# A decoder trunk on one core: the third attention unit is turned by DMA, one step's weights are split first, and GpSimd's work on a convolution channel is put behind another unit's low parts

## The chip, the cores and the metric

The kernel runs on one core of a Trainium2 chip. The core has a matrix engine (TensorE, "PE" in the profile), three engines for elementwise work (VectorE "DVE", ScalarE "ACT", GpSimd "POOL") and a queue engine (SyncE "SP") that issues most transfers. Each engine works its own instruction queue in order; semaphores make one wait for another. The metric is the device time of one execution in microseconds (us), lower is better.

## The reference

Two layers over 512 tokens of width 1024, float32 throughout. Each layer is a half-weighted SwiGLU block, a mixing block and another half-weighted SwiGLU block, with a norm ahead of each. The change lies in the mixing block:

```python
h = rms_norm(x, mix_norm[l])
z = h @ w_in[l]                      # [q | k | v | conv_B | conv_C | conv_h]
# attention: 8 query heads, 2 key/value heads of 64, blocks of 128 tokens,
# each block sees itself and the block before (window 128), ALiBi bias, a learned sink
scores = einsum(qb, k_band) * scale + bias        # masked
m = maximum(max(scores), sink);  p = exp(scores - m)
probs = p / (sum(p) + exp(sink - m))
out = einsum(probs, v_band)
# convolution: B * causal_conv3(C * h_conv), per channel
x = x + concat([attn_out, conv_out]) @ w_out[l]
```

## The kernel before

Every matrix product is made from three products of a short format: both operands are split into a high part (a cast on ScalarE, `wh` for weights) and a low part (the rest, a subtraction on VectorE, `wl`), and high x high, low x high and high x low are summed in PSUM. `split` (line 228) does it for weights; `need_raw` loads them (line 210 on SP), and `need_split(g)` splits all groups up to the g-th. `wh` and `wl` have three buffers each, the loaded weights (`raw`) eight, which they share with the attention's probabilities `p`.

The mixing block goes in steps. One step has a group of 24 products of 128 by 512 columns on TensorE (the function `group`, lines 318 to 321): steps 2 to 5 make the queries, steps 6 to 17 the twelve 128-wide pieces of the convolution's three inputs, in two rounds of six: C for two channels (`cc`, line 1700), h for two channels (`ch`, line 1707, then the three taps), B for two channels (`m`, line 1720). So steps 8 and 9 are `ch` of channels 0 and 1, steps 10 and 11 the products with B. The taps' sum `cc` gets an addition and a product with the norm on GpSimd (lines 1715 and 1716).

Between the groups lies the attention, cut into eight units, one for each block n of 128 tokens and each key/value head g: `p_n_g`, in the order 0_0, 1_0, 2_0, 3_0, 0_1, 1_1, 2_1, 3_1. A unit has four heads with 256 columns of scores (128 for block 0), and these stages:

- `scores`: products of q with the high and low part of k into PSUM (`sc`, lines 1554 and 1555); on VectorE a reduction per head that adds the bias and finds the maximum (line 1558), then `nm`, `es`; on ScalarE four exponentials and one of the sink (`es`, lines 1575 and 1578); on VectorE `sums`, a reciprocal, and the scaling of p (line 1583).
- `turn`: p is needed with keys on the partitions. On TensorE: 128-column transposes into PSUM (`pt`, line 1616). For units 1, 3 and 5 instead by DMA: in `send`, ScalarE lays the two 16-bit halves of each word apart (line 1590, into `crossing`), SP issues a DMA transpose of 16-bit elements back into p (line 1592); in `join`, ScalarE puts the halves together again, one copy for each of the two key blocks (line 1601). Either way each block is then split into `ph` (ScalarE, line 1621) and `pl` (VectorE, line 1622).
- `values`: four products with the values (`o`, lines 1633 and 1634; two for block 0), a copy of the lower half `ol` on ScalarE (line 1636) and additions on VectorE (line 1639).

At which step a unit does what stands in the tables `SCORES_AT`, `SEND_AT`, `TURN_AT`, `VALUES_AT`. `attend(step)` runs the stages of a step; `go_on` calls it, then splits the weights of a group ahead. `INSIDE` names a stage that is run inside a group, between two of its eight k. `tc.issue_after(i)` puts what stands under it behind instruction i. Within these bounds a scheduler orders each engine's instructions, by costs of its own.

PSUM has four accumulators of the kind `mm`, taken in turn by groups (`acc`) and values (`o`), and two each of `sc` and `aux`.

Of the kernel before, what the change touches and what calls it, by code (L numbers as in the profile page):

```python
# [65 lines left out]
SPLIT_AHEAD = 2  # L66
# [9 lines left out]
def trunk_kernel(  # L76
# [23 lines left out]
    nc = tc.nc  # L100
# [519 lines left out]
    norm = Norm(0)  # L620
# [873 lines left out]
    def mix(l, norm, after):  # L1494
# [40 lines left out]
        class Unit:  # L1535
# [49 lines left out]
            def send(self):  # L1585


                self.room = crossing[:, todo.index(self) // 2 % 2, :]
                halves = self.room.bitcast(U16).rearrange("p (two n) -> p two n", two=2)
                nc.scalar.copy(halves, words(self.p.rearrange("p h k -> p (h k)")))  # L1590
# [16 lines left out]
            def turn(self):  # L1607

                self.pt = []
                for kb in range(self.lo // P, 2):  # L1610
                    if todo.index(self) in SEND_AT.values():
                        tp = self.join(kb)
                    else:
                        tp = psum("aux", [P, 4, P], f"pt_{self.name}_{kb}")
                        for h in range(4):
                            nc.tensor.transpose(
                                tp[:, h, :], self.p[:, h, kb * P : (kb + 1) * P], ident
                            )
                    hi = g2(f"ph_{self.name}_{kb}", F32R, (P, 4, P))
                    lo = g2(f"pl_{self.name}_{kb}", F32R, (P, 4, P))  # L1620
                    nc.scalar.copy(hi, tp)
                    last = nc.vector.tensor_sub(lo, tp, f32(hi))
                    self.pt.append((kb, hi, lo))
                return last

# [20 lines left out]
        def attend(step):  # L1646

            done = None
            if step in SEND_AT:
                todo[SEND_AT[step]].send()  # L1650
            for at, stage in ((VALUES_AT, "values"), (TURN_AT, "turn"), (SCORES_AT, "scores")):
                if stage == "turn" and step + 1 == INSIDE[0]:
                    done = todo[VALUES_AT.index(step)].added
                    continue
                if step in at:
                    done = getattr(todo[at.index(step)], stage)() or done
            return done

        for j in range(NH // 2):
# [18 lines left out]
        def product():  # L1678

            def between(k, hi, lo):  # L1680
                if step == INSIDE[0] and k == INSIDE[2]:
                    todo[INSIDE[1]].turn()
# [13 lines left out]
        for pair in range(2):  # L1696
# [7 lines left out]
            for j in range(2):  # L1704
# [7 lines left out]
                nc.vector.scalar_tensor_tensor(  # L1712
                    tap[:, 2:], u[:, : S - 2], conv_of(l, 0, c), tap[:, 2:], op0=ALU.mult, op1=ALU.add
                )
                nc.gpsimd.tensor_add(y[:, 1:], y[:, 1:], tap[:, 1:])
                nc.gpsimd.tensor_mul(y, y, norm.inv)
# [68 lines left out]
```

## Time and profile before

| | us |
|---|---|
| median of 3 runs | 1626.99 |
| lowest, highest | 1626.22, 1627.17 |
| the profiled execution | 1626.19 |
| its span, first to last instruction | 1624.4 |
| TensorE busy | 1615.4 (99%) |
| VectorE, ScalarE, GpSimd busy | 1376.7, 1178.1, 216.5 |
| attention of layer 1, layer 2 | about 363 to 452, 1166 to 1255 |

A row of the timeline is: start (us from the span's start), duration, engine, line, operation, output<-input, shape, count; in brackets, how long the engine stood idle just before and what ended that. Several like rows are merged to "xN". A row of the waits is: who waited, for whom, us in total, times, longest. A row of the windows is: the stretch and its length, then for each engine its busy time and, in brackets, its instructions, then TensorE's granted clock, the share of the DMA engines and GB/s. Matmuls overlap, so their starts tell more than their durations.

### The profile page before, as it was taken

To read this page: it belongs to the slowest core of one execution; us is meant where nothing else is said; L and a number is where in the kernel's file an instruction comes from. 1 tells how busy PE (TensorE), PEld (TensorE's weight loads), DVE (VectorE), ACT (ScalarE), POOL (GpSimd) and SP (SyncE) were. 2 spreads that over 40 slices of the span, in tenths; PEclk is the share of its full clock that TensorE was granted. 3 is DMA by queue.
4 is the path that set the end of the run, shared out by engine and by line. 5 is a ranking of instruction groups with operands and counts; after the bars stand their busy time and mean duration, and the time that the engine had idled before them with its cause. 6 is when DMAs were issued, how large, how long until landed. Compare 5 with 4: busy or idle time off the path is not lost.

```text
span 1624.4 us, 21158 instructions
## 1 busy us (share of the span) xinstructions
PE 1615.4 (99%) x7571; PEld 1349.4 (83%) x7571; DVE 1376.7 (85%) x1788; ACT 1178.1 (73%) x1511; POOL 216.5 (13%) x191
## 2 busy tenths in 40 slices
PE   9999999999999999999999999999999999999998
PEld 7888888888898888888888888888888988888887
DVE  7978798988899977798998777989688998678997
ACT  6677777857766677778866777788586767878665
POOL 1211111001211111111011111110012111111121
PEclk9999999999999999999999999999999999999999
DMA  9999989822597698999767999998136978999892
GB/s 270 212 232 209 220 207 226 233 59 78 143 227 175 177 225 214 218 214 225 218 144 182 224 215 226 215 221 217 42 91 156 233 149 219 225 223 222 241 230 72
DMA packets 306031, 313.92 MB, mean 193 GB/s; under 512 B 125501, under 2 KB 188549, under 8 KB 305925
## 3 DMA queue, kind: packets, MB, share of 16 engines
q1 hardware_dynamic: 265412, 230.90, 50.1%
q0 software_dynamic: 40048, 81.27, 29.3%
q8 instruction: 59, 0.97, 0.2%
q14 instruction: 48, 0.39, 0.1%
q10 hardware_dynamic: 464, 0.40, 0.1%
HBM read 264.29 MB, written 2.10 MB: 164 GB/s over the span
## 4 chain that ended last, share of the span: by engine, by line
PE 98%; DVE 1%; DMA 0%; SPq 0%; issue 0%; ACT 0%; DVEq 0%
PE x L842 27%; PE y L842 13%; PE x_s L842 9%; PE acc L318 7%; PE acc L319 7%; PE acc L321 7%; PE w L842 7%; PE y_s L842 5%; PE x_m L827 3%; PE w_s L842 3%; PE y_m L827 1%; PE y_e L842 1%; PE acc L699 1%; PE x_e L842 1%; PE w_m L827 1%; PE sc L1555 0%
## 5 line engine op out<-in xcount | busy, mean ns | idle before, releaser
L228 DVE TENSOR_TENSOR wl<-raw,wh 128x1024 fp32r<-128x1024 f32 (+1 forms) x494 | 598.6, 1219 | 162.8 <-ACT wh L228 161.9
L228 ACT CAST wh<-raw 128x1024 fp32r<-128x1024 f32 (+1 forms) x494 | 514.1, 1044 | 304.6 <-PE x L842 92.8
L318 PE MATMUL acc<-xh,wh 128*128 128x512 f32 x392 | 153.3, 393 | 0.5 <-ACT wh L228 0.5
L319 PE MATMUL acc<-xl,wh 128*128 128x512 f32 x392 | 153.1, 391 | 0.0
L321 PE MATMUL acc<-xh,wl 128*128 128x512 f32 x384 | 149.7, 390 | 0.0
L223 POOL DMA_DIRECT2D raw<-in_ffn_wu_dram x40 | 50.6, 1272 | 381.6 <-DMA raw<-in_ffn_wu_dram 268.6
L318 PEld LDWEIGHTS acc<-xh,wh 128*128 128x128 f32 x392 | 73.8, 188 | 15.0 <-ACT wh L228 0.6
L319 PEld LDWEIGHTS acc<-xl,wh 128*128 128x128 f32 x392 | 73.7, 188 | 14.5
L321 PEld LDWEIGHTS acc<-xh,wl 128*128 128x128 f32 x384 | 72.1, 188 | 15.3
L223 POOL DMA_DIRECT2D raw<-in_ffn_wd_dram x34 | 41.0, 1218 | 272.0 <-DMA raw<-in_ffn_wd_dram 122.3
L223 POOL DMA_DIRECT2D raw<-in_ffn_wg_dram x40 | 49.1, 1237 | 201.9 <-DMA raw<-in_ffn_wu_dram 84.7
L269 DVE TENSOR_TENSOR raw<-raw,raw 128x1024 f32<-128x1024 f32 x58 | 70.5, 1220 | 1.7 <-DMA raw<-in_ffn_wu_dram 1.2
L1106 ACT COPY raw_a<-turned 128x1024 uint16<-128x1024 uint16 x48 | 63.5, 1357 | 0.0
L842 PE MATMUL x<-wl,ft1h 128*128 128x512 f32 x160 | 62.4, 390 | 0.0
L842 PE MATMUL w<-wh,fb21h 128*128 128x512 f32 x160 | 62.3, 390 | 0.0
L842 PE MATMUL y<-wh,ft3h 128*128 128x512 f32 x160 | 62.3, 390 | 0.0
L842 PE MATMUL x<-wh,ft1l 128*128 128x512 f32 x160 | 62.3, 389 | 0.0
L842 PE MATMUL x<-wl,ft2h 128*128 128x512 f32 x160 | 62.3, 389 | 0.0
L842 PE MATMUL x<-wh,ft2l 128*128 128x512 f32 x160 | 62.3, 389 | 0.0
L842 PE MATMUL x<-wh,ft1h 128*128 128x512 f32 x160 | 62.3, 389 | 0.0
L842 PE MATMUL w<-wh,fb21l 128*128 128x512 f32 x160 | 62.2, 389 | 0.0
L842 PE MATMUL y<-wh,ft3l 128*128 128x512 f32 x160 | 62.2, 389 | 0.0
(517 smaller groups left out, 4545.2 us busy)
## 6 DMA issues: line engine op xcount, KB each, us to landing
raw<-in_ffn_wu_dram SPq DMA_DIRECT2D x127, 512.0 KB, 5.6
raw<-in_ffn_wd_dram SPq DMA_DIRECT2D x105, 512.0 KB, 5.6
raw<-in_ffn_wg_dram SPq DMA_DIRECT2D x86, 512.0 KB, 5.3
raw<-in_ffn_wu_dram POOLq DMA_DIRECT2D x40, 512.0 KB, 9.1
raw<-in_ffn_wg_dram POOLq DMA_DIRECT2D x40, 512.0 KB, 6.5
raw<-in_w_in_dram SPq DMA_DIRECT2D x36, 512.0 KB, 4.0
raw<-in_ffn_wd_dram POOLq DMA_DIRECT2D x34, 512.0 KB, 8.2
raw<-in_w_out_dram SPq DMA_DIRECT2D x20, 512.0 KB, 4.6
```

What stands on the lines that cost most here:

```text
L223: nc.gpsimd.dma_start(out=r, in_=rows_of(*more), accum_op=ALU.add)
L228: return nc.scalar.copy(hi, raw), eng.tensor_sub(lo, raw, f32(hi))
L269: nc.vector.tensor_add(a11, a11, s1)
L318: nc.tensor.matmul(acc, hi[:, k, :], rhs[k][0], start=k == first, stop=False)
L319: nc.tensor.matmul(acc, hi[:, k, :], rhs[k][1], start=False, stop=False)
L321: nc.tensor.matmul(acc, lo[:, k, :], rhs[k][0], start=False, stop=k == last)
L699: nc.tensor.matmul(opening[n], (lo if part == "w" else hi)[:, k, :], xl if part == "x" else xh, start=n not in begun, stop=k == KC - 1 and ...
L827: nc.tensor.matmul(accs[c // 2][:, c % 2, :], w[:, k, cols], x_[:, 2 * h + k, :], start=start and c % 2 == 0 and h + k + i == 0, stop=h + ...
L842: nc.tensor.matmul(accs[u], x_[:, 2 * h + k, tok], w[:, k, :], start=start and h + k + i == 0, stop=h + k == 2 and i == 2, skip_group_chec ...
L1106: nc.scalar.copy(words(raws[self.b][:, c, :]), self.to[:, :, c, :])
```

## The change

Four edits, all in the mixing block.

1. Unit 2_0 (the third) is added to `SEND_AT`, at step 8: its eight TensorE transposes in step 9 go, and it is sent through the DMA. Its words are laid apart by GpSimd (`IDLE_LAYS`), not by ScalarE, and into half of the tile `m_1`, which is not written before the second round, instead of `crossing`. It is turned at step 10 (before: 8) and its values are made at step 11 (before: 9).
2. Unit 1_0's values move into step 11's group, ahead of its k = 3 (before: between steps 10 and 11). Unit 0_1's turn stays in that group at k = 5.
3. At step 9, `go_on` splits the weights of a coming group before the step's attention is recorded, instead of after it.
4. The GpSimd addition and product of channel 1 are recorded after step 9's attention and put behind unit 1_0's low parts (`parted`, the last `pl`).

```diff
-SEND_AT = {7: 1, 9: 3, 11: 5}
-TURN_AT = (6, 9, 8, 11, 10, 13, 14, 15)
-VALUES_AT = (7, 10, 9, 12, 11, 14, 15, 16)
-INSIDE = (11, 4, 5)
+SEND_AT = {7: 1, 8: 2, 9: 3, 11: 5}
+TURN_AT = (6, 9, 10, 11, 10, 13, 14, 15)
+VALUES_AT = (7, None, 11, 12, 11, 14, 15, 16)
+INSIDE = {(11, 3): (1, "values"), (11, 5): (4, "turn")}
+SPLIT_FIRST = 9
+IDLE_LAYS = (2,)
...
-                self.room = crossing[:, todo.index(self) // 2 % 2, :]
+                n = todo.index(self)
+                self.room = crossing[:, n // 2 % 2, :]
+                if n == 2:
+                    self.room = mixed[1][:, 2:4, :].rearrange("p c s -> p (c s)")
                 halves = self.room.bitcast(U16).rearrange("p (two n) -> p two n", two=2)
-                nc.scalar.copy(halves, words(self.p.rearrange("p h k -> p (h k)")))
+                whole = words(self.p.rearrange("p h k -> p (h k)"))
+                (nc.gpsimd.tensor_copy if n in IDLE_LAYS else nc.scalar.copy)(halves, whole)
...
-                    last = nc.vector.tensor_sub(lo, tp, f32(hi))
+                    last = self.parted = nc.vector.tensor_sub(lo, tp, f32(hi))
...
         def go_on():
             nonlocal step
+            if step == SPLIT_FIRST:
+                need_split(state["group"] - 1 + SPLIT_AHEAD)
             last = attend(step)
...
-                nc.gpsimd.tensor_add(y[:, 1:], y[:, 1:], tap[:, 1:])
-                nc.gpsimd.tensor_mul(y, y, norm.inv)
                 ys.append(y)
-                go_on()
+                behind = step == SPLIT_FIRST
+                if behind:
+                    go_on()
+                with tc.issue_after(todo[1].parted.ins) if behind else nullcontext():
+                    nc.gpsimd.tensor_add(y[:, 1:], y[:, 1:], tap[:, 1:])
+                    nc.gpsimd.tensor_mul(y, y, norm.inv)
+                if not behind:
+                    go_on()
```

What it does to the order, in the first layer (the second has the same). Numbers at the end of names tell buffers apart and differ between the two programs, as line numbers do.

On VectorE at steps 8 and 9, before: unit 2_0 and unit 3_0 are handled in turn, with the two subtractions of unit 2_0 (`pl`, from PSUM) and the weights behind `nm_3_0`.

```order
L1712 SCALAR_TENSOR_TENSOR tap_0_3422<-ch_0_0_3394,par,tap_0_3422 128x510
L1622 TENSOR_TENSOR pl_2_0_0_3433<-pt_2_0_0_3427,ph_2_0_0_3432 128x512
L1558 ISA p_3_0_3446,mx_3_0_3445<-sc_3_0_1_3454,bias,sink 128x256
L1558 ISA mx_3_0_3445 128x1
L1622 TENSOR_TENSOR pl_2_0_1_3442<-pt_2_0_1_3436,ph_2_0_1_3441 128x512
L1569 TENSOR_SCALAR nm_3_0_3461<-mx_3_0_3445 128x4
L228 TENSOR_TENSOR wl_3480<-raw_3126,wh_3479 128x1024
```

The same place in the changed kernel:

```order
L1585 TENSOR_SCALAR p_2_0_3357<-p_2_0_3357,sums_2_0_3376 128x256 x4
L1721 SCALAR_TENSOR_TENSOR tap_0_3422<-ch_0_0_3394,par,tap_0_3422 128x510
L1560 ISA p_3_0_3430,mx_3_0_3429<-sc_3_0_1_3438,bias,sink 128x256
L1560 ISA mx_3_0_3429 128x1
L230 TENSOR_TENSOR wl_3501<-raw_3164,wh_3500 128x1024
L1571 TENSOR_SCALAR nm_3_0_3445<-mx_3_0_3429 128x4
L1573 TENSOR_TENSOR es_3_0_3447<-sink,nm_3_0_3445 128x4
```

The two subtractions of 2_0 are gone from here, and weights one group further on (`wl_3501`) now stand ahead of `nm_3_0`; the weights that stood behind `nm_3_0`, from `raw_3126`, stand a step earlier, ahead of `nm_2_0`.

On GpSimd, the changed kernel (before, the first of these rows was not there):

```order
L1596 COPY m_1_2959<-p_2_0_3357 128x2048
L1729 TENSOR_TENSOR cc_0_0_3246<-cc_0_0_3246,tap_0_3422 128x511
L1730 TENSOR_TENSOR cc_0_0_3246<-cc_0_0_3246,inv_3011 128x512
L1729 TENSOR_TENSOR cc_0_1_3320<-cc_0_1_3320,tap_1_3495 128x511
L1730 TENSOR_TENSOR cc_0_1_3320<-cc_0_1_3320,inv_3011 128x512
```

The copy of 2048 16-bit elements reads `p_2_0` as soon as it is scaled, and channel 0's two operations follow it.

On ScalarE at steps 9 to 11, before, from the laying apart of 3_0 to the cast `ph_0_1_1` that `o_0_1` reads:

```order
L1590 COPY crossing_3080<-p_3_0_3446 128x2048
L1621 CAST ph_1_0_1_3533<-crossing_3080 128x512
L228 CAST wh_3644<-raw_3314 128x1024
L228 CAST wh_3704<-raw_3388 128x1024
L1575 ACTIVATE p_0_1_3538,sums_0_1_3557<-p_0_1_3538,nm_0_1_3553 128x128 x4
L1578 ACTIVATE es_0_1_3555<-es_0_1_3555 128x4
L1636 COPY ol_1_0_3606<-o_1_0_3601 64x512
L1601 COPY crossing_3080<-p_3_0_3446 128x2x512 x2
L1621 CAST ph_0_1_1_3669<-pt_0_1_1_3664 128x512
```

and in the changed kernel:

```order
L1577 ACTIVATE p_0_1_3517,sums_0_1_3536<-p_0_1_3517,nm_0_1_3532 128x128 x4
L1580 ACTIVATE es_0_1_3534<-es_0_1_3534 128x4
L1607 COPY m_1_2959<-p_2_0_3357 128x2x512 x2
L1627 CAST ph_2_0_0_3577<-m_1_2959 128x512
L1607 COPY crossing_3080<-p_3_0_3430 128x2x512
L1627 CAST ph_2_0_1_3582<-m_1_2959 128x512
L1607 COPY crossing_3080<-p_3_0_3430 128x2x512
L1642 COPY ol_1_0_3639<-o_1_0_3634 64x512
L1577 ACTIVATE p_1_1_3587,sums_1_1_3606<-p_1_1_3587,nm_1_1_3602 128x256 x4
L1580 ACTIVATE es_1_1_3604<-es_1_1_3604 128x4
L1627 CAST ph_0_1_1_3654<-pt_0_1_1_3649 128x512
```

Between the exponentials of 0_1 and `ph_0_1_1` stand now the joins and casts of unit 2_0 and the exponentials of unit 1_1; before, these exponentials came behind it. On TensorE, the products `o_2_0`, two score products of unit 2_1 and the first product of `o_0_1` now stand behind step 11's group, and the second of `o_0_1` behind the first three products of step 12's.

More of the change, by code (lines that the diff above doesn't have):

```diff
@@ L1651, in attend @@
             for at, stage in ((VALUES_AT, "values"), (TURN_AT, "turn"), (SCORES_AT, "scores")):
[L1652 to L1656, printed above, removed]
+                for n in (n for n, when in enumerate(at) if when == step):
+                    if (n, stage) in INSIDE.values():
+                        done = todo[1].parted
+                    else:
+                        done = getattr(todo[n], stage)() or done
             return done
@@ L1680, in between @@
             def between(k, hi, lo):
-                if step == INSIDE[0] and k == INSIDE[2]:
-                    todo[INSIDE[1]].turn()
+                if (step, k) in INSIDE:
+                    n, stage = INSIDE[step, k]
+                    getattr(todo[n], stage)()
             return group(norm.h, between, own=take_split(SPLIT_AHEAD - 1))
```

## The prediction

> **What bounds the kernel now.** I read the page first, then TensorE's waits, then the attention stage of the first layer (363 to 452 us) engine by engine in the timeline, and two windows to see that the second layer repeats it.
>
> ```profile
> span 1624.4 us, 21158 instructions
> PE 1615.4 (99%) x7571; PEld 1349.4 (83%) x7571; DVE 1376.7 (85%) x1788; ACT 1178.1 (73%) x1511; POOL 216.5 (13%) x191
> ...
> PE 98%; DVE 1%; DMA 0%; SPq 0%; issue 0%; ACT 0%; DVEq 0%
> ```
> ```profile
> PE idle L151 <- DVE warm L646: 1.2, 1, 1.2
> PE xt L665 <- DMA xin<-in_x_dram: 0.6, 1, 0.6
> PE acc L318 <- ACT wh L228: 0.5, 1, 0.5
> ```
> ```profile
> 363.00:452.00 89.00, 89.00 (x441) 74.25 (x440) 73.39 (x195) 63.63 (x131) 15.76 (x12) 1.00 0.42 113
> 1166.00:1255.00 89.00, 89.00 (x444) 74.63 (x443) 74.00 (x196) 64.06 (x131) 15.44 (x12) 1.00 0.42 113
> ```
>
> TensorE carries the time: the chain is 98% PE, its three waits come to 2.3 us, and in both attention windows it is busy for all 89.00 us at clock 1.00 with 441 and 444 products. So this change can win only what it takes off TensorE, and every us in which TensorE waits is lost. VectorE (73.39 of 89) and ScalarE (63.63) have slack on average; what counts is one chain through them.
>
> What the change takes off TensorE, and the place where it will be measured:
>
> ```profile
> 389.81 1.12 PE L1616 MATMUL pt<-ident,p 128*128 128x128 f32 x8
> 390.69 0.48 PE L319 MATMUL acc<-xl,wh 128*128 128x512 f32 x1
> ...
> 403.08 0.39 PE L1633 MATMUL o<-ph,vv 128*128 128x512 f32 x1
> 403.43 0.50 PE L1634 MATMUL o<-pl,vv 128*128 128x512 f32 x1
> ...
> 410.67 0.39 PE L1633 MATMUL o<-ph,vv 128*128 128x512 f32 x1
> 410.90 0.39 PE L1634 MATMUL o<-pl,vv 128*128 128x512 f32 x1
> 411.13 0.39 PE L318 MATMUL acc<-xh,wh 128*128 128x512 f32 x1
> ```
>
> The eight transposes of unit 2_0 hold TensorE from 389.81 to 390.69, 0.88 us, and the product behind takes 0.48 where others take 0.39: 0.97 us. The last product of o_1_0 starts 0.35 behind its neighbour where 0.23 is usual (410.90 to 411.13), since pl_1_0_1 was late: 0.12 us. At 411.13 the group of step 12 begins; I compare the two kernels there.
>
> **The change part by part.** *The bound of the gain.* Without the transposes and that wait TensorE is 0.97 + 0.12 = 1.09 us ahead per layer, 2.2 us in all, if nothing new holds it.
>
> *What now stands behind the new copy.* GpSimd takes over the copy that lays unit 2_0's words apart, 2048 uint16 in a partition, once p_2_0 is scaled. The trace has no such copy on GpSimd. These rows bound it and show what else it does:
>
> ```profile
> 0.27 0.10 POOL L1772 MEMSET const-float32-1.0<- 128x1 f32 x1
> ...
> 0.88 0.21 POOL L171 MEMSET ones<- 128x128 f32 x1
> ...
> 1.36 0.29 POOL L173 CAST ones_r<-ones 128x128 fp32r<-128x128 f32 x1
> 345.04 1.04 POOL L1675 TENSOR_TENSOR inv<-inv 128x512 f32<-128x512 f32 x1 [59.89 <-DVE inv L447]
> ...
> 399.82 1.29 POOL L1715 TENSOR_TENSOR cc<-cc,tap 128x511 f32<-128x511 f32 x1 [4.79 <-issue]
> 401.19 1.63 POOL L1716 TENSOR_TENSOR cc<-cc,inv 128x512 f32<-128x512 f32 x1
> ```
> ```profile
> 385.50 0.17 DVE L1569 TENSOR_SCALAR nm<-mx 128x4 f32<-128x4 f32 x1
> 387.92 0.16 DVE L1579 TENSOR_TENSOR sums<-sums,es 128x4 f32<-128x4 f32 x1 [2.05 <-ACT es L1578]
> 389.19 1.13 DVE L1583 TENSOR_SCALAR p<-p,sums 128x256 f32<-128x256 f32 x4
> 391.48 0.75 DVE L1712 SCALAR_TENSOR_TENSOR tap<-ch,par,tap 128x510 f32<-128x510 f32 x1 [0.34 <-ACT tap L1711]
> 394.98 1.21 DVE L228 TENSOR_TENSOR wl<-raw,wh 128x1024 fp32r<-128x1024 f32 x1
> 400.48 1.18 DVE L1622 TENSOR_TENSOR pl<-crossing,ph 128x512 fp32r<-128x512 f32 x1
> 402.40 0.97 DVE L1622 TENSOR_TENSOR pl<-crossing,ph 128x512 fp32r<-128x512 f32 x1
> 413.88 0.69 DVE L1622 TENSOR_TENSOR pl<-crossing,ph 128x512 fp32r<-128x512 f32 x1
> ```
>
> The same subtraction takes 0.69 us alone (413.88) and 1.18 and 0.97 beside GpSimd. It ends 0.55 behind GpSimd's end both times: 401.66 behind 399.82 + 1.29 = 401.11, and 403.37 behind 401.19 + 1.63 = 402.82. In between GpSimd's own product is the late one, 1.63 for 1.29, and ends 1.16 behind VectorE's 401.66. So of the two, whoever comes second stands until the first is through, if VectorE reads two operands from SBUF. [...]
>
> The length of the copy: the cast of 128 elements takes 0.29, of which the fixed part lies between the 0.10 of a one-column memset and the 0.21 of a memset of the same 128. That leaves 1.5 to 0.6 ns an element, 3.1 to 1.5 us for 2048. ScalarE does the very copy in 1.90 (383.02, below); four times GpSimd's 1.04 for 512 elements of a product is 4.2. I take 2.4, the middle of what GpSimd's own one-operand row gives, with 1.5 and 4.2 as ends. [...] No row here shows a long copy on GpSimd.
>
> *When it runs.* Step 8 now has weights (wl_3464) split ahead of nm_2_0, so nm_2_0 starts about 1.0 later (a wl takes 1.21, and small instructions start just before the end of what stands ahead). The exponentials shift with it, the sums from 387.92 to 389.1 with a score reduction now in front of them, and p_2_0 is scaled from 390.1 to 391.25, 1.0 behind the sums because two more reductions lie between (before: 389.19 to 390.32). tap_0, with two SBUF operands, starts next and ends at 391.9; the copy gets its turn there and ends at 391.9 + 2.4 - 0.14 = 394.2. Next but one on VectorE is wl_3501 with two SBUF operands, ready at 392.2: it stands until 394.2 and ends 1.08 (1.21 - 0.14) later, at 395.3. Behind it in VectorE's queue stand nm_3_0, es_3_0 and ch_0_1; ScalarE's exponentials of unit 3_0 wait for nm_3_0 and start at 395.4.
>
> *The chain on ScalarE.* From there ScalarE never gets free before the unit that TensorE wants next:
>
> ```profile
> 383.02 1.90 ACT L1590 COPY crossing<-p 128x2048 uint16<-128x2048 uint16 x1 [0.30 <-DVE p L1583]
> ...
> 395.10 0.51 ACT L1575 ACTIVATE p<-p,nm 128x256 f32<-128x256 f32 x1 [1.33 <-DVE nm L1569]
> ...
> 397.18 0.71 ACT L1709 ACTIVATE cc<-ch,par 128x512 f32<-128x512 f32 x1
> ...
> 398.52 0.59 ACT L1636 COPY ol<-o 64x512 f32<-64x512 f32 x1
> ...
> 399.53 1.90 ACT L1590 COPY crossing<-p 128x2048 uint16<-128x2048 uint16 x1
> 401.33 0.62 ACT L1621 CAST ph<-crossing 128x512 fp32r<-128x512 f32 x1
> 401.85 1.99 ACT L228 CAST wh<-raw 128x1024 fp32r<-128x1024 f32 x2
> 403.75 0.40 ACT L1575 ACTIVATE p<-p,nm 128x128 f32<-128x128 f32 x1
> ...
> 405.41 0.57 ACT L1636 COPY ol<-o 64x512 f32<-64x512 f32 x1
> 405.88 2.57 ACT L1601 COPY crossing<-p 128x1024 uint16<-128x1024 uint16 x2
> 408.78 0.59 ACT L1621 CAST ph<-pt 128x512 fp32r<-128x512 f32 x1 [0.33 <-PE pt L1616]
> ```
>
> Before, the cast ph_0_1_1 (408.78) ends at 409.37, and o_0_1 runs at 410.67 without waiting. In the new order ScalarE does, from the exponentials of 3_0 to the end of ph_0_1_1, start to start: exponentials and es 2.08; cc and tap 1.34 (397.18 to 398.52); ph 0.5; wh 0.95; lay of 3_0 1.80; ph 0.5; exponentials of 0_1 1.66; two joins of 2_0 2.45; ph 0.5; join 1.23; ph 0.5; join 1.23; ol_1_0 0.47; exponentials of 1_1, now ahead, 2.08; ph_0_1_1 0.59. That is 17.9 us, so ph_0_1_1 ends at 395.4 + 17.9 = 413.3. GpSimd spares ScalarE the 1.90 us that laying 2_0 apart would have cost it; new in ScalarE's list are the two joins (2.45), and the 2.08 that now stand in front of ph_0_1_1.
>
> *The sum.* TensorE comes to o_0_1 at 410.67 - 1.09 + 0.24 (two score products that moved ahead) = 409.8, or a little later, since p_0_1 is scaled late for its transposes. It waits until 413.3, some 3 us, and starts step 12 one product later, 413.5, against 411.13. One product of o_0_1 (0.23) is still owed there, two score products (0.24) are done: even. So +2.4 us a layer, +4.8 in all. The profiled execution took 1626.2 (span 1624.4 and 1.8 around it), the median is 1627.0, 0.8 above; 1627.0 + 4.8 = 1631.8. Each us of the copy is 2 us of the total: 1.5 gives +3.0, 4.2 gives +8.4.
>
> *The other edits.* The convolution's add and product for channel 1 now follow pl_1_0_1: the two subtractions get back 0.49 and 0.28 us of VectorE, which is waiting for ScalarE there, so nothing; their result is done by about 407 and wanted by step 11's product at about 411. Those of channel 0 wait behind the copy and wl_3501 until 395.3 and are done by 398; step 10's product needs them at 404. On SP one more transpose stands ahead of that of 3_0, which is not ready before 402, and ahead of two weight loads whose slots come free with the joins, at 407 and 410; their casts come three steps later. With o_1_0, o_2_0 and o_0_1 together, the accumulator of step 12 is now that of step 11, read by VectorE at about 412: hidden while TensorE waits for ph_0_1_1, late next if that goes.
>
> **The rivals.** [...] *B: not slower, the transposes' time is won.* ScalarE would have to finish ph_0_1_1 by 410, 3.3 us earlier than in my sum; that needs the copy out of the way and 1.5 us of slack in ScalarE's list which I don't see. From 410 on the price is nil, and 1627.0 - 2.2 = 1624.8. *C: the copy is as slow as GpSimd's two-operand rows*, 4.2 us: +8.4, 1635.4. The joins, at 406 and later, would still find their transpose landed. [...] Against it: a copy reads one operand, not two.
>
> **How the numbers follow.** My forecast (copy 1.6 to 3 us) 0.44, C and anything longer 0.18, A 0.22, B 0.16. 0.2% is 3.3 us, about what a measurement here tells from no change; a copy of 1.65 us reaches it. Slower: 0.44 + 0.18 = 0.62. Same: A and B, less a little for what I have not seen, 0.36. Faster by 3.3 us is more than the transposes hold: 0.02. The range from 1627.0 to 1636.5 leaves out B (0.16) and a very long copy. My forecast's own range is 1630.2 to 1633.
>
> **What would show it.** The GpSimd copy as a row of about 2.4 us, followed by a wl of over 3 us that ends 1.08 behind it; ScalarE busy without a gap from the exponentials of 3_0 to ph_0_1_1; a new wait of TensorE, o for ACT ph or an o product 2 to 4 us behind its neighbour, twice; 16 fewer 128-column transposes. I am wrong if wl_3501 takes 1.2 beside the copy, or if TensorE has no wait at o_0_1.

## The result, and the profile after

| | us | ratio to before | 95% interval |
|---|---|---|---|
| before, median of 6 | 1626.63 | | |
| changed, median of 6 | 1634.11 | 1.0048 | 1.0035 to 1.0061 |
| changed, lowest and highest | 1632.60, 1637.18 | | |

The changed kernel is slower by 7.5 us. Its executions scatter over 4.6 us, those of before over 1.5; the profiled one is the slowest, 1637.18 (span 1635.4). So its rows hold 3 us that the median does not have, and where these come from is a part of the finding. All rows are of the first layer unless their times say otherwise.

The page of the changed kernel, and TensorE's waits (who waited for whom, us in total, times, longest):

```profile
span 1635.4 us, 21125 instructions
PE 1619.4 (99%) x7555; PEld 1350.8 (83%) x7555; DVE 1383.1 (85%) x1788; ACT 1182.5 (72%) x1515; POOL 222.8 (14%) x193
...
PE 93%; DVE 2%; ACT 2%; issue 1%; DMA 1%; POOL 0%; SPq 0%; DVEq 0%; POOLq 0%
```
```profile
PE o L1639 <- ACT ph L1627: 5.8, 2, 2.9
...
PE pt L1622 <- DVE p L1585: 0.4, 2, 0.2
```

The 16 transposes are gone (7571 to 7555 products), and TensorE has one new wait per layer, 2.9 us at `o_0_1` for the cast `ph_0_1_1`. TensorE's share of the last chain fell from 98% to 93%.

The timeline of the changed kernel, engine by engine, along the way to that wait:

```profile
391.18 2.27 POOL L1596 COPY m<-p 128x2048 uint16<-128x2048 uint16 x1 [45.27 <-DVE p L1585]
393.42 2.25 POOL L1729 TENSOR_TENSOR cc<-cc,tap 128x511 f32<-128x511 f32 x1
...
390.95 0.75 DVE L1721 SCALAR_TENSOR_TENSOR tap<-ch,par,tap 128x510 f32<-128x510 f32 x1
...
392.02 2.51 DVE L230 TENSOR_TENSOR wl<-raw,wh 128x1024 fp32r<-128x1024 f32 x1
394.45 1.24 DVE L1571 TENSOR_SCALAR nm<-mx 128x4 f32<-128x4 f32 x1
...
395.73 0.51 ACT L1577 ACTIVATE p<-p,nm 128x256 f32<-128x256 f32 x1 [2.29 <-DVE nm L1571]
...
404.47 2.54 ACT L1607 COPY m<-p 128x1024 uint16<-128x1024 uint16 x2
...
410.82 0.50 ACT L1577 ACTIVATE p<-p,nm 128x256 f32<-128x256 f32 x1
...
413.01 0.59 ACT L1627 CAST ph<-pt 128x512 fp32r<-128x512 f32 x1
...
413.64 0.50 PE L1639 MATMUL o<-ph,vv 128*128 128x512 f32 x1 [2.92 <-ACT ph L1627]
413.98 0.40 PE L320 MATMUL acc<-xh,wh 128*128 128x512 f32 x1
414.21 0.39 PE L321 MATMUL acc<-xl,wh 128*128 128x512 f32 x1
...
415.06 0.63 PE L320 MATMUL acc<-xh,wh 128*128 128x512 f32 x1
415.49 0.63 PE L321 MATMUL acc<-xl,wh 128*128 128x512 f32 x1
```

GpSimd and VectorE take turns: the copy runs to 393.45, then `wl_3501` to 394.53 (1.08 behind the copy's end), then channel 0's addition to 395.67, then `nm_3_0` to 395.69. ScalarE, which had nothing to do for 2.29 us, starts unit 3_0's exponentials at 395.73 and is busy from there to the end of `ph_0_1_1` at 413.60. Step 12 begins at 413.98, against 411.13 before: 2.85 us late.

The last two rows are the second loss. Step 12's products come every 0.43 us (415.06 to 415.49), not every 0.23 (413.98 to 414.21). The windows of the changed kernel (stretch, its length, busy time of each engine with its instructions in brackets, then TensorE's granted clock), cut where the clock changes:

```profile
411.28:414.69 3.41, 1.04 (x5) 0.88 (x6) 2.60 (x8) 3.36 (x12) 0.00 (x0) 1.00 0.52 154
414.70:418.11 3.41, 3.41 (x10) 2.67 (x9) 2.24 (x7) 3.26 (x5) 0.00 (x0) 0.50 0.01 2
...
1216.83:1220.24 3.41, 1.17 (x6) 0.65 (x4) 2.16 (x6) 3.41 (x11) 0.00 (x0) 1.00 0.51 149
1220.24:1223.65 3.41, 2.73 (x7) 2.15 (x8) 2.82 (x9) 2.32 (x5) 0.00 (x0) 0.50 0.24 72
1223.65:1227.07 3.42, 3.42 (x10) 2.65 (x9) 1.52 (x3) 3.42 (x4) 0.00 (x0) 0.50 0.00 1
```

Behind each wait the clock is halved, for 3.41 us in layer 1 and for twice that in layer 2. At the granted 0.50, 3.41 us hold the work of 1.7, so each halved window costs an estimated 1.7 us, and up to 5 us of the profiled execution's 10.6 are the clock's; a part of layer 2's falls into the wait itself. The mean clocks of the executions say roughly how often it happens: one halved window is 0.001 of the mean, but the profiled executions of the two kernels also end at half speed, for 3.9 us (before) and 2.2 (changed), which are about 0.001 as well. The slowest execution, 1637.18, has 0.996; four, from 1633.93 to 1635.36, have 0.998; the fastest, 1632.60, has 0.999, which is what the kernel before has in nearly all. If that one was spared, the waits alone cost about 6.0 us (1632.60 against 1626.63), and the halved clock about 1.5 in the median. The kernel touch2 below bears this out: its profiled execution has the full clock behind like waits and takes 6.2 us more than before.

### The profile page after: what moved, and what is told of

It reads as the page before. It is cut to its first block, busy times and chain, and to the rows that moved or that the text cites. A ratio compares the mean times of both kernels' runs of the same rounds, so it can differ in the third digit from the quotient of the medians.

```text
span 1635.4 us, 21125 instructions
## 1 busy us (share of the span) xinstructions
PE 1619.4 (99%) x7555; PEld 1350.8 (83%) x7555; DVE 1383.1 (85%) x1788; ACT 1182.5 (72%) x1515; POOL 222.8 (14%) x193
## 4 chain that ended last, share of the span: by engine, by line
PE 93%; DVE 2%; ACT 2%; issue 1%; DMA 1%; POOL 0%; SPq 0%; DVEq 0%; POOLq 0%
PE x L844 27%; PE y L844 13%; PE x_s L844 9%; PE w L844 7%; PE acc L320 7%; PE acc L321 7%; PE acc L323 6%; PE y_s L844 5%; PE w_s L844 3%; PE x_m L829 2%; PE y_m L829 1%; PE y_e L844 1%; PE acc L701 1%; PE x_e L844 1%; DVE wl L230 1%
## 5 line engine op out<-in xcount | busy, mean ns | idle before, releaser
L844 PE MATMUL w<-wl,fb21h 128*128 128x512 f32 x160 | 62.2, 389 | 0.0
L844 PE MATMUL x<-wl,fb11h 128*128 128x512 f32 x160 | 62.2, 389 | 0.0
```

The source lines that it names most:

```text
L844: nc.tensor.matmul(accs[u], x_[:, 2 * h + k, tok], w[:, k, :], start=start and h + k + i == 0, stop=h + k == 2 and i == 2, skip_group_chec ...
```

## The experiments

All twelve kernels below were timed beside the kernel before, whose medians lay between 1626.37 and 1626.58. "The builder" in the expectations is the scheduler that orders each engine's instructions within the bounds the code sets. "The port" there is a name for GpSimd and VectorE holding each other up, as `wl_3501` shows above (2.51 us beside GpSimd's copy; another batch of low parts takes 1.22 at 385.21 in the same profile); what in the hardware does it no run shows. Where two kernels are said to have the same order, their instruction lists are equal on every engine, but for the instructions that the edit itself adds, takes out or moves.

### The clock and the place of one cast

*fill12* puts idle products into the wait:

```diff
                 o = op.rearrange("p a b q -> p (a b q)")
+                if todo.index(self) == 4:
+                    spin(12, o)
```

> The changed kernel with twelve idle products on TensorE ahead of o_0_1 (into o_0_1's own bank, overwritten after), 12 x 0.23 = 2.7 us of the wait of 2.9 us; what ScalarE does ahead of ph_0_1_1 is as before. Theory 1 (the 2.9 us wait halves TensorE's clock afterwards, and that is what the forecast lacked): the products of step 12 still begin near 414, but come every 0.23 us, the granted clock stays at 1.0 there, and the time falls by the 1.7 us of layer 1 and about as much or up to 3.1 us in layer 2: 1628.5 to 1631. Rival 1 (the halved clock has another cause, or costs nothing at the end): the clock falls all the same and the time stays within 1 us of 1634.1.

Measured: 1637.75 us, ratio 1.0072 [1.0059, 1.0084]. All five executions have clock 0.999, so the clock half of theory 1 holds, but the time went up, not down, and is in neither expectation. The timeline of this kernel:

```profile
410.76 2.54 PE L153 MATMUL o<-zero 128*128 128x512 bf16 x11
413.83 0.50 PE L1641 MATMUL o<-ph,vv 128*128 128x512 f32 x1 [0.54 <-ACT ph L1627]
```

Step 13 begins at 422.26 instead of 422.89, but the scheduler counted the idle products as time and also ordered ScalarE and VectorE otherwise behind them, which costs 1.7 us from there to the end of layer 1 and 1.9 in layer 2. The run shows that a filled wait keeps the clock up; what that saves it does not show.

*exps_late* moves `ph_0_1_1` ahead of unit 1_1's exponentials on ScalarE, by making these a stage of their own:

```diff
-                sums = small(f"sums_{self.name}")
+                self.rows = nm, es
+                if todo.index(self) != 5:
+                    self.soften()
+            def soften(self):
+                lo, (nm, es) = self.lo, self.rows
+                sums = small(f"sums_{self.name}")
...
                     getattr(todo[n], stage)()
+                    if n == 4:
+                        todo[5].soften()
```

> The changed kernel with one cast of ScalarE moved: ph_0_1_1 ahead of unit 1_1's exponentials instead of behind them. GpSimd's copy and additions and VectorE's wait for them stay. Theory 2 (the wait at o_0_1 is ScalarE's order: 2.19 us of unit 1_1's exponentials stand ahead of the cast that TensorE waits for; the port only adds 0.6 us): ph_0_1_1 begins at 410.8 and ends at 411.4, TensorE waits about 0.8 us instead of 2.9, step 12 begins at 411.8 instead of 414.0, and with no halved clock behind it the time falls by 2 x 2.2 plus 1.7 and 1.7 to 3.1: 1625.5 to 1627.5. Rival 2 (the port's hold on VectorE is the cause): exponentials of 3_0 still start at 395.7, other waits take over within step 11 or 12, and the time stays above 1630.

Measured: 1633.84 us, 1.0043 [1.0031, 1.0056]: theory 2 missed by 6 us. The time is where rival 2 has it, above 1630, and other waits took over as it says; whether GpSimd's hold on VectorE is the reason is asked with *no_copy*. The timeline of this kernel, and behind it the start of step 13 in the kernel before:

```profile
411.39 0.58 ACT L1633 CAST ph<-pt 128x512 fp32r<-128x512 f32 x1
...
412.02 0.50 PE L1645 MATMUL o<-ph,vv 128*128 128x512 f32 x1 [1.08 <-ACT ph L1633]
413.02 0.49 PE L1646 MATMUL o<-pl,vv 128*128 128x512 f32 x1 [0.49 <-DVE pl L1634]
...
419.92 0.50 PE L1645 MATMUL o<-ph,vv 128*128 128x512 f32 x1 [0.24 <-ACT ph L1633]
```
```profile
418.43 0.40 PE L318 MATMUL acc<-xh,wh 128*128 128x512 f32 x1
```

The cast did come 1.6 us earlier and the long wait broke up, but `ph_3_0_1`, which the next values need, still ends at 419.9 (415.8 before), and step 13 begins at 421.82 against 418.43. Here, putting one piece of ScalarE's work ahead of another only moved the place where TensorE waits.

### Parts of the change alone

*lay_scalar* is one table entry, `IDLE_LAYS = ()`: ScalarE lays unit 2_0 apart.

> The changed kernel with unit 2_0's copy on ScalarE instead of GpSimd: nothing holds VectorE from 391 to 393.4, ScalarE has 1.9 us more. The builder then also moves one of unit 1_0's joins behind the exponentials of 3_0 and puts ph_0_1_1 ahead of unit 1_1's exponentials. Theory 2: nm_3_0 comes by 394.0, but the exponentials of 3_0 start no earlier than 394 since ScalarE has the copy; what matters is ph_0_1_1 ahead of the exponentials: the wait at o_0_1 is under 1.5 us, no halved clock, 1626 to 1629. Rival 2 (the port): the exponentials of 3_0 start 2 us earlier than 395.7 and the time falls below 1626.

Measured: 1632.80 us, 1.0039 [1.0025, 1.0053]. Neither time came. There is no wait at `o_0_1` left, but one of unit 1_0's joins, now late, makes VectorE idle for 1.97 us, and TensorE waits for a score reduction of unit 0_1 instead:

```profile
PE sc L1556 <- DVE mx L1560: 4.7, 2, 2.4
```

And `nm_3_0` began no earlier than 394.26, without the copy: counted from the start of `tap_0`, the exponentials of 3_0 start 4.46 us later here (391.08 to 395.54) and 4.78 in the changed kernel (390.95 to 395.73). The copy's whole effect on them is 0.3 us. Nor does laying apart on GpSimd save ScalarE time that counts: in the changed kernel ScalarE stands idle for 2.29 us just before these exponentials, and here its own copy (1.88 us, at 392.21) lies in that gap.

*turn_alone* keeps the turn by DMA and takes back the two small parts:

```diff
-SPLIT_FIRST = 9
+SPLIT_FIRST = None
...
-                behind = step == SPLIT_FIRST
+                behind = False
```

> The changed kernel with unit 2_0's turn by DMA alone: GpSimd's copy stays, but step 9's weights are split at their old place and channel 1's work is put back ahead of step 9's attention. GpSimd's copy and addition still hold VectorE (exponentials of 3_0 near 395 to 395.7), and the builder puts ph_0_1_1 ahead of unit 1_1's exponentials. Theory 2: no long wait at o_0_1, the clock stays up, 1626 to 1629. Rival 2 (the port): the copy's hold alone keeps the time above 1630.

Measured: 1631.35 us, 1.0029 [1.0018, 1.0041]. It loses less than the whole change. The time is above 1630, as rival 2 has it, but not for its reason: the exponentials of 3_0 are early, and neither theory named the wait that is there. The timeline of this kernel:

```profile
391.17 2.27 POOL L1596 COPY m<-p 128x2048 uint16<-128x2048 uint16 x1 [45.29 <-DVE p L1585]
...
392.13 1.33 DVE L1571 TENSOR_SCALAR nm<-mx 128x4 f32<-128x4 f32 x1
...
393.50 0.51 ACT L1577 ACTIVATE p<-p,nm 128x256 f32<-128x256 f32 x1
...
404.00 0.71 PE L323 MATMUL acc<-xh,wl 128*128 128x512 f32 x1 [1.87 <-DVE wl L230]
```

With the same copy on GpSimd, `nm_3_0` ends at 393.46 and the exponentials of 3_0 start at 393.50, 2.23 us earlier than in the changed kernel: there, it is the weights split first, `wl_3501` ahead of `nm_3_0`, that make them late. In exchange these weights, step 11's, now come late themselves, and TensorE waits 1.87 us for them.

*small_parts* is the kernel before with the two small parts alone:

```diff
+SPLIT_FIRST = 9
...
+            if step == SPLIT_FIRST:
+                need_split(state["group"] - 1 + SPLIT_AHEAD)
...
+                behind = step == SPLIT_FIRST
...
+                with tc.issue_after(todo[1].parted.ins) if behind else nullcontext():
```

> The kernel before with the two small parts alone: step 9's weights split first, and channel 1's addition and product put behind the attention of step 9. Unit 2_0 is still turned by TensorE, GpSimd has no copy. Theories 2 and 3: no joins are added, so nothing of the loss is here: within 1.5 us of 1626.4. If the small parts carried a part of the loss (kernel with the turn alone measured 1631.35 against 1634.1 with them): 1628 to 1630.

Measured: 1630.61 us, 1.0025 [1.0016, 1.0035]. More than half of the loss is here, without the third unit's transposing DMA, joins or copy, so theories 2 and 3 fall. The two losses do not add up, though: the turn alone costs 5.0 us and the split alone 4.1, and both together 7.5, so on top of the turn the split costs 2.8. TensorE's new wait in small_parts:

```profile
PE o L1634 <- ACT ph L1622: 3.2, 2, 1.6
```

Built one by one, the split alone gives the same order as both small parts, and channel 1's GpSimd work put behind gives the order of before; the same holds on top of the turn by DMA. So channel 1's place did nothing, and the 4.1 us are the split's.

*small_late* asks whether they hang on `ph_0_1_1`, which the scheduler put behind unit 1_1's exponentials there:

```diff
                     todo[INSIDE[1]].turn()
+                    todo[5].soften()
```

> The kernel with the two small parts alone, with ph_0_1_1 ahead of three of unit 1_1's four exponentials on ScalarE instead of behind all four. Theory 4 (splitting step 9's weights first costs 4.1 us only because the builder then puts ph_0_1_1 behind the exponentials of 1_1, 2.19 us, and TensorE waits for it): ph_0_1_1 ends 1.6 us earlier, no wait over 0.3 us at o_0_1, and the time is within 1 us of 1626.5. Theory 3 alone (ScalarE's load; the order of two works in it does not matter, as in the changed kernel with the exponentials late): 1630 to 1631 again.

Measured: 1630.82 us, 1.0026 [1.0017, 1.0036]. No gain; theory 4 falls, and the time is where theory 3 has it. The timeline of this kernel shows where ScalarE loses time, and behind it stand two rows of the kernel before:

```profile
396.14 1.21 DVE L229 TENSOR_TENSOR wl<-raw,wh 128x1024 fp32r<-128x1024 f32 x1
397.27 0.68 DVE L1717 TENSOR_TENSOR ch<-acc,cc 128x512 f32<-128x512 f32 x1
...
397.98 0.72 ACT L1719 ACTIVATE cc<-ch,par 128x512 f32<-128x512 f32 x1 [0.76 <-DVE ch L1717]
...
409.46 1.22 DVE L229 TENSOR_TENSOR wl<-raw,wh 128x1024 fp32r<-128x1024 f32 x1
410.59 0.17 DVE L1570 TENSOR_SCALAR nm<-mx 128x4 f32<-128x4 f32 x1
...
410.79 0.51 ACT L1582 ACTIVATE p<-p,nm 128x256 f32<-128x256 f32 x1 [1.15 <-DVE nm L1570]
```
```profile
396.18 0.68 DVE L1707 TENSOR_TENSOR ch<-acc,cc 128x512 f32<-128x512 f32 x1
...
408.59 0.17 DVE L1569 TENSOR_SCALAR nm<-mx 128x4 f32<-128x4 f32 x1
```

A second batch of low parts stands ahead of `ch_0_1` (before, one) and, later, a batch ahead of `nm_1_1` (before, behind it). They start 1.1 and 2.0 us later than before, and each time ScalarE stands idle behind them (0.76 and 1.15 us). So the split does its harm here at other instructions than in the changed kernel: `nm_3_0` still stands ahead of the weights.

### The joins, the copy and its hold

*no_join* leaves out the two joins of unit 2_0:

```diff
+                if todo.index(self) in IDLE_LAYS:
+                    return self.turned[:, kb * 4 * P : (kb + 1) * 4 * P].rearrange("p (h q) -> p h q", h=4)
                 whole = self.room[:, kb * 4 * P : (kb + 1) * 4 * P]
```

> The changed kernel without the two joins of unit 2_0 on ScalarE (2 x 1.27 = 2.54 us per layer); the casts behind them read the transposed halves as they are, so unit 2_0's values are left out of the result. The builder also puts ph_0_1_1 ahead of unit 1_1's exponentials. Theory 3 (formed on the runs before this: any order of ScalarE's work leaves step 12 at 413.4 to 414.9, since ScalarE is full from 395 to 414, and what fills it are the joins that the turn by DMA adds): step 12 begins at 411.3 or earlier, no wait over 0.8 us at o_0_1, and 1624.5 to 1627.5. Rival 2 (the port: GpSimd's copy holds VectorE and with it nm_3_0): the copy is still there, so the chain stays late whatever ScalarE does, and the time stays above 1629.5.

Measured: 1629.76 us, 1.0016 [1.0007, 1.0025], all clocks 0.999 or 1.0. The time is where rival 2 has it, above 1629.5, and theory 3 misses it by 2.3 us; but rival 2's reason fails too, since the chain did not stay late:

```profile
411.49 0.50 PE L1642 MATMUL o<-pl,vv 128*128 128x512 f32 x1 [0.45 <-DVE pl L1630]
411.83 0.40 PE L320 MATMUL acc<-xh,wh 128*128 128x512 f32 x1
```

Step 12 begins at 411.83, 2.15 us earlier than in the changed kernel, and the wait at `o_0_1` is 0.45 us. So the joins, with what hangs on them (the place of `ph_0_1_1` and the clock), are 4.35 of the 7.5 us, and no window behind a wait is slowed in its profile. Step 13 begins at 419.43, still 1.0 late.

*pool_join* gives the joins to GpSimd, all other orders as in no_join:

```diff
-                    nc.scalar.copy(
+                    (nc.gpsimd.tensor_copy if todo.index(self) in IDLE_LAYS else nc.scalar.copy)(
```

> The changed kernel with the two joins of unit 2_0 on GpSimd instead of ScalarE; all other orders are those of the kernel without the joins. GpSimd's copy of 2048 uint16 took 2.27, so a join of 1024 is about 1.15 to 1.3 if the strided side costs nothing. Theory 3: ScalarE is as free as without the joins, so the time is that of the kernel without them plus what GpSimd's two copies hold VectorE for, up to 2.4 us per layer: 1625 to 1631. Rival 2 (the port is the main cause): two more holds of VectorE in the stage make it worse than the changed kernel: above 1634.

Measured: 1633.48 us, 1.0042 [1.0029, 1.0054]. The time lies between the two expectations. Two copies of 1.47 and 1.35 us on GpSimd cost 3.7 us in all against no_join, which has the same order on the other engines: VectorE's `tap_1` takes 1.79 beside the first, and TensorE waits up to 1.9 us for scaled probabilities. That is 1.86 us a layer; how much of it is GpSimd and VectorE holding each other up and how much the clock (0.997 to 0.999 here) is not separated.

*no_copy* leaves out GpSimd's copy as well (the DMA transposes unit 2_0's rows as they are); the rest has the same order:

```diff
-                (nc.gpsimd.tensor_copy if n in IDLE_LAYS else nc.scalar.copy)(halves, whole)
...
+                if n in IDLE_LAYS:
+                    nc.sync.dma_start_transpose(
+                        self.room.bitcast(U16).rearrange("p (c q) -> p c q", q=P), self.turned
+                    )
```

> The kernel without the joins, and without GpSimd's copy too: the transposing DMA reads unit 2_0's rows as they are (its values are left out of the result as there); every other instruction stands in the same order on every engine. It measures what the forecast put at the centre, the copy's hold on VectorE. The forecast's step (the copy holds wl_3501 to 1.08 behind its end, nm_3_0 follows, and the exponentials of 3_0 start late by as much): wl_3501 ends near 393.2, the exponentials of 3_0 start 0.7 to 1.3 us earlier than 395.7, and the time falls from 1629.76 by 1.4 to 2.6: 1627.2 to 1628.4. If the hold is hidden: 1629.3 to 1630.2. If the copy was all of what is left: 1624.5 to 1625.5.

Measured: 1629.04 us, 1.0016 [1.0007, 1.0025]. That lies between what the forecast's step gives and what a hidden hold gives. The copy that the forecast rested on is worth 0.7 us of the total, with the executions of each kernel scattering over 2 us. Why so little, in the timeline of this kernel:

```profile
391.85 1.29 POOL L1737 TENSOR_TENSOR cc<-cc,tap 128x511 f32<-128x511 f32 x1 [45.95 <-DVE tap L1729]
393.21 2.14 POOL L1738 TENSOR_TENSOR cc<-cc,inv 128x512 f32<-128x512 f32 x1
...
392.03 2.19 DVE L230 TENSOR_TENSOR wl<-raw,wh 128x1024 fp32r<-128x1024 f32 x1
394.14 1.24 DVE L1571 TENSOR_SCALAR nm<-mx 128x4 f32<-128x4 f32 x1
...
395.41 0.51 ACT L1577 ACTIVATE p<-p,nm 128x256 f32<-128x256 f32 x1 [1.98 <-DVE nm L1571]
```

Channel 0's addition takes the copy's place in holding `wl_3501` (which ends 1.08 behind it again), and its product that of the addition in holding `nm_3_0`. The exponentials start at 395.41 instead of the changed kernel's 395.73, with `tap_0` at 390.96 and 390.95; lay_scalar, which has the joins, shows the same 0.3 us.

*lay3_pool* moves a second laying apart, unit 3_0's, to GpSimd: `IDLE_LAYS = (2, 3)`.

> The changed kernel with unit 3_0's laying apart on GpSimd too (1.89 us less on ScalarE near 400.5, 2.3 us more on GpSimd). Theory 3 with the port's price as measured (the two joins on GpSimd instead of left out cost 1629.76 to 1633.48, so 1.86 us per layer for two copies of half this size): the gain of 1.89 and the price of 1.86 cancel, 1633 to 1635. ScalarE's load alone, with the port free of charge: 1630 to 1631. The port the main cause: above 1636.

Measured: 1636.10 us, 1.0058 [1.0044, 1.0072], clocks 0.996 and 0.997. The time is just where the third expectation has it, above 1636, but it does not show the hold between GpSimd and VectorE to be the main cause: three halved windows, up to 5 us, are in the profiled execution. The copy takes 2.95 us there, `p_0_1` is scaled late, and TensorE waits 3.4 us for it in each layer:

```profile
399.83 2.95 POOL L1596 COPY crossing<-p 128x2048 uint16<-128x2048 uint16 x1 [2.62 <-DVE p L1585]
```

No kernel tried was as fast as before.

*no_join_alone* takes the joins out of turn_alone, with no_join's edit:

> The turn by DMA alone (weights of step 9 split at their old place, channel 1's work at its old place), with the two joins of unit 2_0 left out as in the kernel without the joins. In the turn alone the exponentials of 3_0 already start at 393.5, 2.2 us before the changed kernel's, GpSimd's copy there or not, and TensorE's one wait is 1.9 us per layer for a low weight part of step 10 (VectorE at 404.6). Theory 5 (two causes and no third: the weights split ahead of nm_3_0, and the joins on ScalarE): with neither, nothing is left but TensorE's saved transposes: 1624.3 to 1626.8. Rival 5 (the turn alone has its own cause on VectorE: the low parts that the DMA releases stand ahead of step 10's weights, joins or not): the wait for the low weight part stays at 1.5 us or grows, and the time is 1629 to 1633.

Measured: 1630.71 us, 1.0026 [1.0017, 1.0035]. Theory 5 falls; rival 5's wait and time came. The waits of this kernel:

```profile
PE acc L323 <- DVE wl L230: 3.7, 2, 1.9
```

The wait of turn_alone is still there to the hundredth (1.87; the low weight part is step 11's, not step 10's as the expectation has it), and the joins, which come behind it, were never its cause.

### The clock once more

*touch2* puts two short products into the changed kernel's wait, released by VectorE's results; the orders of the other engines stay:

```diff
+                if todo.index(self) == 4:
+                    for done in (mixed[0][:, 0, P : 2 * P], mixed[1][:, 1, :P]):
+                        nc.tensor.transpose(o[:, :P], done, ident)
```

> The changed kernel with two short products (128x128, into o_0_1's own bank, overwritten after) in TensorE's wait at o_0_1: one is released by unit 1_0's output near 411.8, the other by channel 1's output near 412.5, so that no stretch of the wait is longer than about 1.3 us; the orders of the other engines are the changed kernel's own, and two of the products of sc_2_1_0 that stood ahead of o_0_1 stand behind step 12. Theory 1 (a wait of 2.9 us in one piece halves TensorE's clock for 3.4 or 6.8 us): step 12 still begins near 414.0, the granted clock stays 1.0 behind it, and the time is 1.5 to 4 us under the changed kernel's 1634.1: 1630 to 1632.5. Rival 1 (the clock does not hang on the unbroken wait): 0.85 and 0.53 again behind 414, and 1633.5 to 1635.

Measured: 1634.76 us, 1.0045 [1.0033, 1.0058]. The median is where rival 1 has it. The profiled execution (1632.71) has a full clock, but the mean clocks go from 0.999 to 0.997, as the changed kernel's do: 1632.71 and 1633.11 with 0.999, 1634.76 to 1635.47 below. So, by these mean clocks and not by a profile, a wait broken into pieces halves the clock too, in some executions and not in others. With the full clock, step 13 begins at 421.80, 1.1 us earlier than in the changed kernel's profile. What decides is seen when the windows are cut at the clock's own beat: the half-speed stretches in the attention stages, which five of the profiles have, last 3.41 or 6.83 us, and the second layer's begin a whole number of 3.413 us behind the first's (236 beats in the changed kernel and in turn_alone, 237 in lay3_pool). In the changed kernel the first begins 120 beats behind the first record of the full clock, at 5.10 us. This kernel, then turn_alone, then pool_join, in that beat:

```profile
409.08:412.49 3.41, 1.99 (x8) 1.07 (x6) 2.36 (x8) 3.41 (x9) 0.00 (x0) 1.00 0.52 154
412.50:415.91 3.41, 2.34 (x10) 1.82 (x11) 2.64 (x9) 3.36 (x10) 0.00 (x0) 1.00 0.42 125
```
```profile
400.71:404.12 3.41, 1.54 (x12) 1.11 (x11) 3.41 (x5) 3.41 (x12) 0.96 (x1) 1.00 0.68 154
404.12:407.54 3.42, 3.42 (x9) 2.68 (x10) 3.42 (x11) 3.42 (x5) 0.00 (x0) 0.50 0.55 162
```
```profile
1211.52:1214.93 3.41, 1.79 (x7) 1.12 (x7) 3.41 (x6) 3.41 (x4) 0.98 (x1) 1.00 0.11 21
1214.94:1218.35 3.41, 3.17 (x15) 2.57 (x16) 3.40 (x15) 1.31 (x3) 0.00 (x0) 1.00 0.83 237
```

In touch2 the loss of TensorE time falls on both sides of a beat (busy 1.99 and 2.34 of 3.41), and the granted clock stays at 1.00. A window with 1.54 us busy is followed by half speed, one with 1.79 is not. In all fourteen profiles it is so, between 395 and 428 us and between 1198 and 1236: after each of the ten full-speed windows in which TensorE was idle for 1.87 us or more comes a halved one, after none with 1.63 or less. So in these profiles the edge lies between 1.63 and 1.87. The first record of the full clock stands at 6.04 us in the profile before and at 5.10 in the changed kernel's, so the beat falls differently on the work of the two. That it also shifts between executions of one kernel, so that the same wait halves the clock in one and not in another, no run shows: it would fit the scatter, but only one execution of each kernel has a profile.

## Why the prediction was right, and where it was not

1634.1 was measured, 1631.8 forecast: slower as forecast and inside the stated range, but outside the forecast's own, 1630.2 to 1633. By its steps:

- *What bounds the kernel, and the place.* Right: every us that TensorE waits is lost, and the one new wait is at `o_0_1`, for `ph_0_1_1`, in both layers. Step 12 began at 413.98, the forecast had 413.5; the wait is 2.92 us, the forecast "some 3" (3.5 by its own 409.8 and 413.3; TensorE came to `o_0_1` only at 410.7, having waited for `p_0_1` before its transposes, which the forecast put at "a little later").
- *The chain on ScalarE.* Right: 17.9 us forecast, 395.73 to 413.60 is 17.87, almost without a gap. That the two joins count is borne out in the main by no_join: 4.35 us less without them, for 2 x 2.45 forecast. That GpSimd "spares ScalarE the 1.90 us" is right as a count and wins nothing: ScalarE stood idle for 2.29 us just there.
- *The copy and when it runs.* Its row is 2.27 us long against 2.4, but it begins at 391.18, beside `tap_0` (390.95 to 391.70), where the forecast had it wait for `tap_0`'s end. It ends 1.75 us behind that end, and in lay3_pool (402.78) again 1.75 behind the end of VectorE's last instruction with two operands (401.03). If the copy stood until these were through, as the forecast has it of whoever comes second, its own length by the forecast's reckoning is 1.75 + 0.14, about 1.9 us: an estimate, as no row shows the copy without such a neighbour. The forecast's end for `wl_3501`, 1.08 behind the copy's, held to the hundredth (394.53 behind 393.45). Unforeseen was that channel 0's addition then holds `nm_3_0`, which has one operand: it took 1.24 us for four columns, where `nm_1_1` takes 0.16 (409.86). The forecast kept the hold to instructions with two; the rows of the kernel before show it at `nm_3_0` as well, which took 0.66 at 394.40 and ended 0.03 behind GpSimd's product (395.06 behind 393.74 + 1.29). The exponentials at 395.73, where the forecast has 395.4, are so in part luck: the copy ended 0.75 us early (393.45, not 394.2), and the addition's hold put 1.1 on top.
- *What the copy is worth.* Wrong. "Each us of the copy is 2 us of the total" would make a copy of 2.27 us 4.5 us (3.8 by the estimate of 1.9); without it the time fell by 0.7 (no_copy against no_join), and the exponentials came 0.3 us earlier with the joins there too (lay_scalar). The forecast compared a kernel whose VectorE is held by the copy with one in which nothing holds it. With the copy gone, GpSimd's next instructions hold it: `wl_3501` still takes 2.19 us in no_copy.
- *The other edits.* The weights split first are in the forecast's reading ("next but one on VectorE is wl_3501"), and their place ahead of `nm_3_0` is in its 395.4; but it puts that lateness down to the copy and gives the split no price of its own. Alone the split costs 4.1 us (small_parts), on top of the turn 2.8; in the changed kernel it puts the exponentials of 3_0 2.2 us later than the turn alone has them, with the same copy on GpSimd. For channel 1's work "nothing" is right, but not as described: it does not come to stand behind `pl_1_0_1`. Its addition starts at 400.41, that subtraction at 402.94, and the order is the one without the edit.
- *The sum.* +2.4 us a layer was forecast at step 12, and 2.85 measured. What is missing is what comes behind the wait: TensorE's clock is not in the forecast. About 6.0 us of waits (the fastest execution) stand against the forecast's 4.8, and the halved clock brings the median to 7.5.
- *The rivals.* A, with its 0.22 for a copy that does not hold `wl_3501`, is false: the copy did hold it (2.51 us, ending 1.08 behind the copy). B, a gain, did not come in any kernel: with joins and copy both left out it is still 2.6 us slower than before. C is false, 2.27 us is not 4.2.

What stays open: the changed kernel with the weights' low parts pinned behind `nm_3_0` and the joins on an engine with room was not built; pool_join and lay3_pool show that GpSimd is not that engine here. How much of the 4.35 us that the joins are worth is the clock was not separated; the changed kernel's own scatter puts it at 1.5.

## What to carry to other kernels

Where three engines hand each other short instructions without slack, an operation has no price of its own: find what would be late if it were taken out, since the next one in the queue can hold the same place, as channel 0's addition did in no_copy and lay_scalar. A split or a copy moved "ahead" is put ahead of something; look at which small instruction (a maximum's negative, a scale) stands behind it and who waits for that. And TensorE's waits that came to 1.87 us or more within one 3.41 us beat of its clock were paid twice here, the second time by a halved clock behind them, an estimated 1.7 us for each halved beat; count such waits in the trace, and look at the clock of every execution before a scatter is called noise.

## What the runs showed of the hardware that was not expected

TensorE's granted clock fell to half behind waits of 1.87 us (turn_alone) and 2.92 us, for one or two beats of 3.41 us. The beat shows in the changed kernel's clock records, 3.413 and 6.827 us long, and in the starts of the halved stretches of all five profiles that have them. In no window was TensorE idle throughout (the most was 3.10 of 3.41 us, in lay3_pool), and 1.87 us was enough. In the two cases in which the halved window was itself idle for 0.68 us (changed kernel, layer 2) and 0.72 (lay3_pool), the half speed lasted a second one; in the other eight it was busy throughout, and full speed followed.

GpSimd's copy of 2048 16-bit elements took 2.27 us at 391 us, with VectorE's `tap_0` (two operands) running beside its first half us, and 2.95 at 399.8 in lay3_pool, with two such instructions beside it. Both end 1.75 us behind the last of these. On the other side, `nm_3_0`, an instruction of four columns that takes 0.16 us at `nm_1_1` (409.86), took 1.24 and 1.33 us (changed kernel, turn_alone) and ended both times 0.02 us behind GpSimd's addition or copy: standing second made it eight times as long.
